# First modulation in quarters with the weights as stationary operand, and first key products over the channels in a fixed order

## The chip, the cores and the metric

The kernel runs on one core of a Trainium2 chip. TensorE multiplies (its weight loads are listed as PEld), VectorE (DVE), ScalarE (ACT) and GpSimd (POOL) do elementwise work, SyncE (SP) issues most DMAs. The metric is the device time in microseconds (us); lower is better. Three runs of the kernel before took 2928.11 to 2932.33 us, median 2929.12.

## What is computed

One layer of a diffusion backbone over 1024 tokens (64 x 16 grid) of 1024 channels, with 256 context tokens. The change touches the first step of all:

```python
def modulate(x, g, shift, scale):
    return rmsnorm(x, g) * (1 + scale) + shift

mod = silu(cond) @ ada_w + ada_b          # ada_w: 1024 x 6144; sh1, sc1, ... are 1024 columns each
h  = modulate(x,   norm1_g, sh1,  sc1)    # cond = c
hc = modulate(ctx, norm1_g, sh1c, sc1c)   # cond = c_ctx
p  = h @ w_in                             # columns 0 to 1023 are the keys
```

What follows (neighbourhood attention, Fourier and pooling mixers, gated merge, 16 experts of which each takes 128 tokens, final norm) is the same in both kernels.

## The kernel before

`start` (L179) brings everything up to the first key products. Its parts:

- *Modulation* (`modulation`, L216). The columns of shift and scale, 2048, come in four chunks of 512, each as two DMAs of 1 MB (rows of 2 KB). Both conditionings (`cs`, 2 columns) are done at once. In each half chunk, two of the four channel blocks go to TensorE with `cs` as stationary operand and 512 moving columns (L223), the other two are multiplied and summed on VectorE (L228, L230), and a matmul with ones (L233) adds these sums over the partitions. The result has 2 partitions, so it is copied (L235) and turned by four small transposes (L238) into one PSUM bank `mps` with the channels on the partitions. When all four chunks are done, L283 and L284 make `mod` (shift, scale) and `A` = g (1 + scale).
- *x* (`load`, `normed`). Four tiles of 128 tokens are loaded (L247), squared and summed on ScalarE (L249), scaled by their root mean square (L257) and turned by TensorE (L261), 4 transposes to each of the 8 channel blocks, two PSUM banks in rotation; ScalarE copies each bank out (L277, L289). This is done for each half of the tokens (x0 and x1). The four buffers `xt` serve both halves, so x1's loads wait for x0's transposes.
- *h* (`modulated`, L265). For each half and channel block k, `hT` gets a high part (L267, ScalarE) and a low part (L273, VectorE), from an unrounded value (L271, or ScalarE L269 for k = 2 and 5).
- *Keys* (`keys`, L309; `projT`, L300). For each half of the tokens and each of four blocks of 128 key columns, one PSUM bank gathers 8 channel blocks x 3 products (`mm3`: high x high, L67; high x low, L68; low x high, L69). A block therefore needs all eight channel blocks of `hT` before it can end. The weights come as two DMAs of 1 MB and are split into a high part on ScalarE (L62) and a low part; for this first chunk the low part is made on GpSimd.

A scheduler decides the order on every engine from the order of the program, its own estimate of times, and the buffers (three `wraw` for raw weights, four `whl` for split ones, two of which first hold the turned x). Each engine then keeps its order; SP issues DMAs in order too, so one that waits for a buffer holds those behind it.

Of the kernel before, what the change touches and what calls it, by code (L numbers as in the profile page):

```python
# [19 lines left out]
D = 1024  # L20
SEQ = 1024
# [13 lines left out]
def f(ap):  # L35
    return ap.bitcast(F32)


class Kernel:
# [75 lines left out]
    def run(self, upto=99):  # L115
        nc, tc, io = self.nc, self.tc, self.io
        with ExitStack() as st:
# [18 lines left out]
            self.queue = [lambda: self.wchunk(w_in, K_OFF, eng=nc.gpsimd)]  # L136
            self.queue += [cols(c) for c in (K_OFF + 512, V_OFF, V_OFF + 512, F_OFF, Q_OFF, Q_OFF + 512)]
# [3 lines left out]
            with ExitStack() as s1:  # L141
# [4 lines left out]
                self.hT = self.hpool.tile([128, 2, KT, SEQ], F32R, name="hT")  # L146
                with self.pool("kvq") as kvq:
                    self.hcT = kvq.tile([128, 2, KT, CTX], F32R, name="hcT")
                    self.keys_values(self.start())
# [29 lines left out]
    def start(self):  # L179
        nc, io = self.nc, self.io  # L180
        const, ps = self.const, self.ps
        with self.pool("startp", 2) as sp:
# [29 lines left out]
            ones = sp.tile([128, 3], F32, name="ones", bufs=1)  # L212
            nc.gpsimd.memset(ones, 0.0)
            nc.gpsimd.memset(ones[:, 1:2], 1.0)

            def modulation(ch):  # L216
                mp = ps.tile([128, 512], F32, name="mm")
                for hf in range(2):
                    raw = self.wraw.tile([128, 2048], F32, name="wraw")
                    rv = raw.rearrange("p (k c) -> p k c", c=512)  # L220
                    nc.sync.dma_start(rv, aw[:, 4 * hf:4 * hf + 4, 512 * ch:512 * ch + 512])
                    for k in range(2):
                        nc.tensor.matmul(mp[:2], cs[:, 4 * hf + k, :], rv[:, k],  # L223
                                         start=hf == k == 0, stop=False)
                    for w in range(2):
                        if hf == 0:
                            accs[w] = sp.tile([128, 512], F32, name=f"acc{w}", bufs=1)
                            nc.vector.tensor_scalar_mul(accs[w], rv[:, 2], cs[:, 2, w:w + 1])  # L228
                        for k in range(3 if hf == 0 else 2, 4):
                            nc.vector.scalar_tensor_tensor(accs[w], rv[:, k], cs[:, 4 * hf + k, w:w + 1], accs[w],  # L230
                                                           op0=ALU.mult, op1=ALU.add)
# [46 lines left out]
            for ch in range(1, 4):  # L278
                modulation(ch)
# [1145 lines left out]
```

## Time and profile before

| | us |
|---|---|
| median of 3 runs | 2929.12 |
| the profiled execution | 2928.25 |
| its span, first to last instruction | 2926.5 |
| first key product (L67) starts | 48.31 |
| TensorE turns to the context (first transpose of its tokens) | 100.20 |

A row of the timeline gives start, duration, engine, line, operation, output<-input and, in brackets, idle time of the engine before it and what ended it. A row with xN merges N instructions, and its duration runs from the first one's start to the last one's end. A matmul's own duration holds its latency, so the pitch between starts is what a product costs. An fp32 matmul is listed as two instructions, one of fp32r (the h and weight parts) as one.

### The profile page before, as it was taken

To read this page: it belongs to the slowest core of one execution; us is meant where nothing else is said; L and a number is where in the kernel's file an instruction comes from. 1 tells how busy PE (TensorE), PEld (TensorE's weight loads), DVE (VectorE), ACT (ScalarE), POOL (GpSimd) and SP (SyncE) were. 2 spreads that over 40 slices of the span, in tenths; PEclk is the share of its full clock that TensorE was granted. 3 is DMA by queue.
4 is the path that set the end of the run, shared out by engine and by line. 5 is a ranking of instruction groups with operands and counts; after the bars stand their busy time and mean duration, and the time that the engine had idled before them with its cause. 6 is when DMAs were issued, how large, how long until landed. Compare 5 with 4: busy or idle time off the path is not lost.

```text
span 2926.5 us, 36071 instructions
## 1 busy us (share of the span) xinstructions
PE 2811.0 (96%) x13607; PEld 2304.4 (79%) x13607; DVE 2040.7 (70%) x2412; ACT 1686.5 (58%) x2005; POOL 280.2 (10%) x436
## 2 busy tenths in 40 slices
PE   7999999999999789987999999999999999999996
PEld 3888888887788777766888888888888888888885
DVE  4423232245578773478888988888888888988887
ACT  5412122212078771245777777777777777777775
POOL 1110000001144320000000000000000000000000
PEclk9999999999999899998999999999999999999998
DMA  8433231225877748558999999999999999999994
GB/s 250 175 124 144 79 123 66 104 80 167 272 190 193 184 140 284 156 166 309 338 362 369 375 367 360 370 376 365 358 367 382 365 361 360 385 364 360 362 383 175
DMA packets 346351, 783.54 MB, mean 268 GB/s; under 512 B 17288, under 2 KB 61008, under 8 KB 346048
## 3 DMA queue, kind: packets, MB, share of 16 engines
q1 hardware_dynamic: 326272, 713.48, 69.3%
q0 software_dynamic: 19664, 67.60, 6.9%
q8 instruction: 107, 1.75, 0.2%
q14 instruction: 68, 0.56, 0.1%
q10 hardware_dynamic: 240, 0.16, 0.0%
HBM read 710.37 MB, written 70.80 MB: 267 GB/s over the span
## 4 chain that ended last, share of the span: by engine, by line
PE 46%; ACT 4%; DVE 2%; issue 1%; DMA 1%; DVEq 0%
PE y L69 5%; PE y L68 5%; PE y L67 5%; PE w_gate L69 5%; PE w_gate L68 5%; PE w_gate L67 5%; PE w_up L67 5%; PE w_up L69 5%; PE w_up L68 5%; ACT whl L62 2%; PE tp L1202 1%; ACT a L1132 1%; ACT xT L1128 1%; DMA wraw<-in_w_up 1%; PE tp L1101 0%
## 5 line engine op out<-in xcount | busy, mean ns | idle before, releaser
L63 DVE TENSOR_TENSOR whl<-wraw,whl 128x2048 fp32r<-128x2048 f32 (+1 forms) x656 | 1295.1, 1997 | 240.4 <-ACT whl L62 236.3
L62 ACT CAST whl<-wraw 128x2048 fp32r<-128x2048 f32 (+1 forms) x660 | 1092.1, 1671 | 445.0 <-PE y L69 132.5
L68 PE MATMUL mm<-hT,whl 128*128 128x512 f32 x768 | 300.9, 392 | 1.6 <-DVE hT L273 1.6
L67 PE MATMUL mm<-hT,whl 128*128 128x512 f32 x768 | 300.2, 392 | 1.5 <-ACT hT L267 1.5
L69 PE MATMUL mm<-hT,whl 128*128 128x512 f32 x768 | 300.8, 392 | 0.0
L69 PE MATMUL w_gate<-whl,xT 128*128 128x512 f32 (+1 forms) x768 | 290.8, 379 | 2.8 <-DVE xT L1133 2.8
L67 PE MATMUL w_gate<-whl,xT 128*128 128x512 f32 (+1 forms) x768 | 292.1, 380 | 0.0
L67 PE MATMUL w_up<-whl,xT 128*128 128x512 f32 (+1 forms) x768 | 291.5, 380 | 0.0
L68 PE MATMUL w_gate<-whl,xT 128*128 128x512 f32 (+1 forms) x768 | 289.7, 377 | 0.0
L69 PE MATMUL w_up<-whl,xT 128*128 128x512 f32 (+1 forms) x768 | 289.1, 376 | 0.0
L68 PE MATMUL w_up<-whl,xT 128*128 128x512 f32 (+1 forms) x768 | 288.4, 375 | 0.0
L67 PE MATMUL y<-whl,aT 128*128 128x512 f32 x704 | 284.8, 405 | 0.0
L69 PE MATMUL y<-whl,aT 128*128 128x512 f32 x704 | 278.7, 396 | 0.0
L68 PE MATMUL y<-whl,aT 128*128 128x512 f32 x704 | 278.1, 395 | 0.0
L67 PEld LDWEIGHTS mm<-hT,whl 128*128 128x128 f32 x768 | 144.9, 189 | 37.8 <-ACT sg L529 5.2
L69 PEld LDWEIGHTS w_gate<-whl,xT 128*128 128x128 f32 x768 | 145.2, 189 | 32.2 <-DVE xT L1133 3.5
L68 PEld LDWEIGHTS mm<-hT,whl 128*128 128x128 f32 x768 | 145.3, 189 | 31.7 <-DVE hT L273 2.1
L69 PEld LDWEIGHTS mm<-hT,whl 128*128 128x128 f32 x768 | 145.2, 189 | 30.1
L68 PEld LDWEIGHTS w_gate<-whl,xT 128*128 128x128 f32 x768 | 145.0, 189 | 29.6
L69 PEld LDWEIGHTS w_up<-whl,xT 128*128 128x128 f32 x768 | 144.5, 188 | 29.1
L67 PEld LDWEIGHTS w_gate<-whl,xT 128*128 128x128 f32 x768 | 144.8, 189 | 28.4
L68 PEld LDWEIGHTS w_up<-whl,xT 128*128 128x128 f32 x768 | 144.3, 188 | 28.3
(354 smaller groups left out, 4333.1 us busy)
## 6 DMA issues: line engine op xcount, KB each, us to landing
wraw<-in_w_gate SPq DMA_DIRECT2D x160, 1024.0 KB, 11.1
wraw<-in_w_up SPq DMA_DIRECT2D x160, 1024.0 KB, 9.0
wraw<-in_w_down SPq DMA_DIRECT2D x160, 1024.0 KB, 11.8
wraw<-in_w_in SPq DMA_DIRECT2D x28, 1024.0 KB, 5.5
wraw<-in_ada_w SPq DMA_DIRECT2D x24, 1024.0 KB, 6.3
wraw<-in_w_gate SPq DMA_DIRECT2D x32, 512.0 KB, 11.4
wraw<-in_w_up SPq DMA_DIRECT2D x32, 512.0 KB, 8.5
wraw<-in_w_down SPq DMA_DIRECT2D x32, 512.0 KB, 4.9
```

The lines of the kernel that those rows point to most:

```text
L62: self.nc.scalar.copy(hi, src)
L63: (eng or self.nc.vector).tensor_sub(lo, src, f(hi))
L67: mm(out, lh, rh, start=start, stop=False, **kw)
L68: mm(out, lh, rl, start=False, stop=False, **kw)
L69: mm(out, ll, rh, start=False, stop=stop, **kw)
L1128: nc.scalar.activation(ex.xT[:, 0, kk], tp[:, cs], AF.Identity, bias=B, scale=A)
L1132: nc.scalar.activation(h32[:, cs], tp[:, cs], AF.Identity, bias=B, scale=A)
L1202: nc.tensor.transpose(tp[:, 128 * k:128 * k + 128], ex.ready[:, 128 * k:128 * k + 128], self.ident)
```

## The change

The modulation is done by quarters. Quarter q holds shift and scale for two channel blocks, 2q and 2q+1: four DMAs of 512 KB (rows of 1 KB) instead of two of 1 MB. `affine(q)` multiplies with the 128x128 blocks of `ada_w` as stationary operand and the two columns of `cs` as moving one, 4 x 8 matmuls, straight into `mps` with the channels on the partitions. VectorE's sums, the ones, the copy and the small transposes are gone. `mod` and `A` of those two channel blocks follow at once. The quarters' raw data lie in places not yet in use: quarter 0 in `hcT`'s, 1 and 2 in the second half of `hT` (which becomes two tiles, class `Halves`), 3 in two `wraw` buffers.

x0 is loaded ahead of the weights. The key products of the first token half run over the channels: four PSUM banks are open together, and quarter q of the loop adds channel blocks 2q and 2q+1 to all four. After the second bank of quarters 0 to 2 the next `affine` stands, and x1's transposes stand in quarter 2. All this is fixed in the written order on TensorE (`manual_schedule`). The copies of turned x alternate between ScalarE and VectorE, as do the scalings; the low part of the first weights is made on VectorE.

```diff
--- before.py
+++ after.py
@@ -36,6 +36,21 @@
     return ap.bitcast(F32)
 
 
+class Halves:
+
+
+    def __init__(self, pool):
+        self.pool, self.tiles = pool, [None, None]
+
+    def take(self, half):
+        self.tiles[half] = self.pool.tile([128, 2, KT, 512], F32R, name=f"hT{half}")
+
+    def __getitem__(self, at):
+        p, s, k, t = at
+        half = t.start // 512
+        return self.tiles[half][p, s, k, t.start - 512 * half:t.stop - 512 * half]
+
+
 class Kernel:
 
 
@@ -133,8 +148,7 @@
-            self.queue = [lambda: self.wchunk(w_in, K_OFF, eng=nc.gpsimd)]
...
+                self.hT = Halves(self.hpool)
                 with self.pool("kvq") as kvq:
-                    self.hcT = kvq.tile([128, 2, KT, CTX], F32R, name="hcT")
-                    self.keys_values(self.start())
+                    self.keys_values(self.start(kvq))
...
-    def start(self):
+    def start(self, kvq):
...
-            ones = sp.tile([128, 3], F32, name="ones", bufs=1)
-            nc.gpsimd.memset(ones, 0.0)
-            nc.gpsimd.memset(ones[:, 1:2], 1.0)
-
-            def modulation(ch):
-                mp = ps.tile([128, 512], F32, name="mm")
+            mv = mps[:, :32].rearrange("p (c w) -> p w c", w=2)
+
+            def columns(q):
+
+
+                if q < 3:
+                    if q == 0:
+                        raw = kvq.tile([128, KT, 512], F32, name="hcT")
+                    else:
+                        raw = later[:, q - 1]
+                    parts = [raw[:, 0:4], raw[:, 4:8]]
+                else:
+                    parts = [self.wraw.tile([128, 2048], F32, name="wraw").rearrange("p (k c) -> p k c", c=512)
+                             for _ in range(2)]
                 for hf in range(2):
-                    raw = self.wraw.tile([128, 2048], F32, name="wraw")
-                    rv = raw.rearrange("p (k c) -> p k c", c=512)
-                    nc.sync.dma_start(rv, aw[:, 4 * hf:4 * hf + 4, 512 * ch:512 * ch + 512])
-                    for k in range(2):
-                        nc.tensor.matmul(mp[:2], cs[:, 4 * hf + k, :], rv[:, k],
-                                         start=hf == k == 0, stop=False)
-                    for w in range(2):
-                        if hf == 0:
-                            accs[w] = sp.tile([128, 512], F32, name=f"acc{w}", bufs=1)
-                            nc.vector.tensor_scalar_mul(accs[w], rv[:, 2], cs[:, 2, w:w + 1])
-                        for k in range(3 if hf == 0 else 2, 4):
-                            nc.vector.scalar_tensor_tensor(accs[w], rv[:, k], cs[:, 4 * hf + k, w:w + 1], accs[w],
-                                                           op0=ALU.mult, op1=ALU.add)
-                for w in range(2):
-                    nc.tensor.matmul(mp[:2], ones[:, 1 - w:3 - w], accs[w], start=False, stop=w == 1)
-                modr = sp.tile([2, 512], F32, name="modr", bufs=1)
-                nc.scalar.copy(modr, mp[:2])
+                    for s in range(2):
+                        c0 = D * s + 256 * q
+                        nc.sync.dma_start(parts[hf][:, :, 256 * s:256 * s + 256], aw[:, 4 * hf:4 * hf + 4, c0:c0 + 256])
+                return parts
+
+            def affine(q, parts):
+
                 for j in range(4):
-                    ct = 4 * ch + j
-                    nc.tensor.transpose(mps[:, 2 * ct:2 * ct + 2], modr[:, 128 * j:128 * j + 128],
-                                        self.ident[:2, :2])
-
-            accs = [None, None]
+                    ct = 8 * (j // 2) + 2 * q + j % 2
+                    for k in range(KT):
+                        nc.tensor.matmul(mps[:, 2 * ct:2 * ct + 2], parts[k // 4][:, k % 4, 128 * j:128 * j + 128],
+                                         cs[:, k], start=k == 0, stop=k == KT - 1)
+                both = lambda c: cols[:, c:c + 2].rearrange("p (o c) -> p o c", o=1).to_broadcast([128, 2, 2])
+                for o in (2 * q, 8 + 2 * q):
+                    nc.vector.tensor_add(mod[:, :, o:o + 2], mv[:, :, o:o + 2], both(o))
+                nc.vector.scalar_tensor_tensor(A[:, :, 2 * q:2 * q + 2], mod[:, :, 8 + 2 * q:10 + 2 * q], 1.0,
+                                               both(16 + 2 * q), op0=ALU.add, op1=ALU.mult)
 
             def load(src, n):
                 xs, ss = [], sp.tile([128, n], F32, name=f"ss{n}")
@@ -250,12 +265,19 @@
                     xs.append(xt)
                 return xs, ss
 
-            def normed(xs, ss, put):
+            def normed(xs, ss):
                 n = len(xs)
                 r = self.rstd(ss, sp, f"rs{n}")
                 for i in range(n):
-                    nc.scalar.activation(xs[i], xs[i], AF.Identity, scale=r[:, i:i + 1])
-                for k in range(KT):
+                    if i % 2:
+                        nc.vector.tensor_scalar_mul(xs[i], xs[i], r[:, i:i + 1])
+                    else:
+                        nc.scalar.activation(xs[i], xs[i], AF.Identity, scale=r[:, i:i + 1])
+                return xs
+
+            def turned(xs, ks, put):
+                n = len(xs)
+                for k in ks:
                     tp = ps.tile([128, 512], F32, name="tp", bufs=2)
                     for i in range(n):
                         nc.tensor.transpose(tp[:, 128 * i:128 * i + 128],
@@ -272,28 +294,72 @@
                                             op0=ALU.mult, op1=ALU.add)
                 (nc.gpsimd if k in () else nc.vector).tensor_sub(lo, h32, f(hi))
 
-            modulation(0)
+            wv = io["w_in"].rearrange("(k p) c -> p k c", p=128)[:, :, K_OFF:K_OFF + 512]
+            wr, wp = [], []
+
+            def wload(s):
+                wr.append(self.wraw.tile([128, 2048], F32, name="wraw"))
+                nc.sync.dma_start(wr[s].rearrange("p (k c) -> p k c", c=512), wv[:, 4 * s:4 * s + 4])
+
+            def wsplit(s):
+                hl = self.whl.tile([128, 2, 2048], F32R, name="whl")
+                for a in (0, 1024):
+                    self.split(hl[:, 0, a:a + 1024], hl[:, 1, a:a + 1024], wr[s][:, a:a + 1024])
+                wp.append(hl.rearrange("p s (k c) -> p s k c", c=512))
+
+            W = lambda s, k: wp[k // 4][:, s, k % 4]
+            put = lambda half: lambda k, p: (nc.vector.tensor_copy if k % 2 else nc.scalar.copy)(xn(k, half), p)
+            later = self.hpool.tile([128, 2, KT, 512], F32, name="hT1")
+            self.hT.take(0)
             x0 = load(lambda i: xv[i], 4)
-            normed(*x0, lambda k, p: nc.scalar.copy(xn(k, 0), p))
-            for ch in range(1, 4):
-                modulation(ch)
-            W = self.next(0)
-            mv = mps[:, :32].rearrange("p (c w) -> p w c", w=2)
-            for w in range(2):
-                nc.vector.tensor_add(mod[:, w, :], mv[:, w, :], cols[:, 0:16])
-                nc.vector.scalar_tensor_tensor(A[:, w, :], mod[:, w, 8:16], 1.0, cols[:, 16:24],
-                                               op0=ALU.add, op1=ALU.mult)
+            ada = [columns(0)]
+            wload(0)
+            ada.append(columns(1))
+            wload(1)
+
+            order = ExitStack()
+            order.enter_context(self.tc.manual_schedule(engines={mybir.EngineType.PE}))
+            affine(0, ada[0])
+            turned(normed(*x0), range(KT), put(0))
             x1 = load(lambda i: xv[4 + i], 4)
-            for half in range(2):
-                if half:
-                    normed(*x1, lambda k, p: nc.scalar.copy(xn(k, 1), p))
-                for k in range(KT):
-                    ts = slice(512 * half, 512 * half + 512)
-                    modulated(self.hT[:, 0, k, ts], self.hT[:, 1, k, ts], xn(k, half), k, 0)
-            for half in range(2):
-                self.keys(W, sp, 0, self.hT, 512 * half, 512, 512 * half)
+            ada += [columns(2), columns(3)]
+            wsplit(0)
+
+            acc = []
+
+            def shifted(q):
+                for k in (2 * q, 2 * q + 1):
+                    modulated(self.hT[:, 0, k, 0:512], self.hT[:, 1, k, 0:512], xn(k, 0), k, 0)
+
+            shifted(0)
+            x1 = normed(*x1)
+            for q in range(4):
+                for blk in range(4):
+                    if q == 0:
+                        acc.append(ps.tile([128, 512], F32, name="mm"))
+                    bs = slice(128 * blk, 128 * blk + 128)
+                    for k in (2 * q, 2 * q + 1):
+                        self.mm3(acc[blk], W(0, k)[:, bs], W(1, k)[:, bs],
+                                 self.hT[:, 0, k, 0:512], self.hT[:, 1, k, 0:512], k == 0, k == KT - 1)
+                    if blk == 1 and q < 3:
+                        affine(q + 1, ada[q + 1])
+                        shifted(q + 1)
+                        if q == 0:
+                            wsplit(1)
+                        if q == 2:
+                            turned(x1, range(4), put(1))
+                if q == 2:
+                    turned(x1, range(4, KT), put(1))
+                    self.hT.take(1)
+            for blk in range(4):
+                self.key_rows(sp, blk, acc[blk], 0)
+            for k in range(KT):
+                modulated(self.hT[:, 0, k, 512:1024], self.hT[:, 1, k, 512:1024], xn(k, 1), k, 0)
+            self.keys(W, sp, 0, self.hT, 512, 512, 512)
+            order.close()
             xc = load(lambda i: io["ctx"][128 * i:128 * i + 128], 2)
-            normed(*xc, lambda k, p: modulated(self.hcT[:, 0, k], self.hcT[:, 1, k], p, k, 1))
+            self.hcT = kvq.tile([128, 2, KT, CTX], F32R, name="hcT")
+            turned(normed(*xc), range(KT), lambda k, p: modulated(self.hcT[:, 0, k], self.hcT[:, 1, k], p, k, 1))
             return W
 
 
@@ -308,11 +374,13 @@
 
     def keys(self, W, sp, ch, src, t0, N, o0):
         for blk in range(4):
-            p = self.projT(W, blk, src, t0, N)
-            hl = sp.tile([128, 2, 512], F32R, name="khl", bufs=2)
-            self.split(hl[:, 0, :N], hl[:, 1, :N], p)
-            c0 = 512 * ch + 128 * blk
-            self.nc.gpsimd.dma_start(self.kd[c0:c0 + 128, :, o0:o0 + N], f(hl[:, :, :N]))
+            self.key_rows(sp, 4 * ch + blk, self.projT(W, blk, src, t0, N), o0)
+
+    def key_rows(self, sp, blk, p, o0):
+        N = p.shape[1]
+        hl = sp.tile([128, 2, 512], F32R, name="khl", bufs=2)
+        self.split(hl[:, 0, :N], hl[:, 1, :N], p)
+        self.nc.gpsimd.dma_start(self.kd[128 * blk:128 * blk + 128, :, o0:o0 + N], f(hl[:, :, :N]))
 
     def keys_values(self, W):
         nc, io = self.nc, self.io
```

TensorE at the start of the program, before (L223 and L233 are the modulation, L238 its turning, L261 transposes of x):

```order
L193 MATMUL mm<-ident,rows 128x48
L223 MATMUL mm<-wraw,cs 2x512 x4
L233 MATMUL mm<-acc_125,ones 2x512
L233 MATMUL mm<-acc_128,ones 2x512
L238 MATMUL mm<-ident,modr 128x2 x4
L223 MATMUL mm<-wraw,cs 2x512 x2
L261 MATMUL tp<-ident,xt 128x128 x2
L223 MATMUL mm<-wraw,cs 2x512
L261 MATMUL tp<-ident,xt 128x128 x2
L223 MATMUL mm<-wraw,cs 2x512
```

The same place after (L250 is `affine`, L283 transposes of x, L82 to L84 the three products of `mm3`; `hcT` is where quarter 0 lies, `hT_116` the first half of h):

```order
L206 MATMUL mm<-ident,rows 128x48
L250 MATMUL mm<-cs,hcT 128x2 x32
L283 MATMUL tp<-ident,xt 128x128 x32
L82 MATMUL mm<-hT_116,whl 128x512
L83 MATMUL mm<-hT_116,whl 128x512
L84 MATMUL mm<-hT_116,whl 128x512
```

The modulation was mixed with x's transposes; now one quarter and all 32 transposes stand ahead of the first product, and the other quarters behind it.

TensorE among the key products of the first half, before:

```order
L261 MATMUL tp<-ident,xt 128x128 x2
L69 MATMUL mm<-hT,whl 128x512
L67 MATMUL mm<-hT,whl 128x512
L68 MATMUL mm<-hT,whl 128x512
L69 MATMUL mm<-hT,whl 128x512
L261 MATMUL tp<-ident,xt 128x128 x8
L67 MATMUL mm<-hT,whl 128x512
```

And after, in the third quarter of the loop (`wraw` is where quarter 3 lies):

```order
L83 MATMUL mm<-hT_116,whl 128x512
L84 MATMUL mm<-hT_116,whl 128x512
L250 MATMUL mm<-cs,wraw 128x2 x32
L283 MATMUL tp<-ident,xt 128x128 x16
L82 MATMUL mm<-hT_116,whl 128x512
L83 MATMUL mm<-hT_116,whl 128x512
```

The transposes of x1 stood in groups of 2 to 8 between products; now 16 of them follow the 32 matmuls of a quarter without a product between, and a second 16 stand a little later.

SP's queue, before (L221 the modulation's weights, L247 x and context, L77 weights of `w_in`):

```order
L221 DMA wraw<-in_ada_w 128x4x512 x2
L247 DMA xt<-in_x 128x1x1024 x4
L221 DMA wraw<-in_ada_w 128x4x512 x6
L77 DMA wraw<-in_w_in 128x4x512
L247 DMA xt<-in_x 128x1x1024
L77 DMA wraw<-in_w_in 128x4x512
L247 DMA xt<-in_x 128x1x1024 x3
L77 DMA wraw<-in_w_in 128x4x512 x3
L247 DMA xt<-in_ctx 128x1024 x2
```

And after (L242 the quarters, L262 x and context, L302 and L92 weights of `w_in`; `hT_115` is the space of quarters 1 and 2):

```order
L262 DMA xt<-in_x 128x1x1024 x4
L242 DMA hcT<-in_ada_w 128x4x256 x4
L302 DMA wraw<-in_w_in 128x4x512
L242 DMA hT_115<-in_ada_w 128x4x256 x4
L302 DMA wraw<-in_w_in 128x4x512
L262 DMA xt<-in_x 128x1x1024 x4
L242 DMA hT_115<-in_ada_w 128x4x256 x4
L242 DMA wraw<-in_ada_w 128x4x256 x4
L92 DMA wraw<-in_w_in 128x4x512 x3
L262 DMA xt<-in_ctx 128x1024 x2
```

x0 moved ahead of all weights; quarters 2 and 3 stand behind x1.

## Rows read from the trace of the kernel before

**Rows 1.** The head of the page.

```profile
span 2926.5 us, 36071 instructions
```

**Rows 2.** Busy time by stage (windows); columns: stretch, length, busy of each engine, clock, DMA.

```profile
0.00:48.31 48.31, 31.42 (x98) 8.47 (x98) 22.34 (x46) 22.11 (x34) 4.06 (x10) 0.93 0.89 279
48.31:57.00 8.69, 7.08 (x19) 5.30 (x20) 3.91 (x5) 5.87 (x9) 5.96 (x3) 0.61 1.03 255
57.00:100.00 43.00, 43.00 (x207) 35.47 (x206) 24.86 (x46) 33.01 (x50) 5.36 (x8) 1.00 0.58 209
```

**Rows 3.** The timeline round the first key products and round the turn to the context.

```profile
48.31 1.20 PE L67 MATMUL mm<-hT,whl 128*128 128x512 f32 x4 [1.48 <-ACT hT L267]
...
51.12 0.79 PE L68 MATMUL mm<-hT,whl 128*128 128x512 f32 x1 [1.61 <-DVE hT L273]
...
92.04 0.39 PE L67 MATMUL mm<-hT,whl 128*128 128x512 f32 x1
...
92.72 0.39 PE L67 MATMUL mm<-hT,whl 128*128 128x512 f32 x1
...
100.20 0.60 PE L261 MATMUL tp<-ident,xt 128*128 128x128 f32 x4
```

**Rows 4.** Groups of TensorE by line and form, first 101 us.

```profile
L223 PE MATMUL mm<-wraw,cs 128*2 128x512 f32 x32 | 18.5, 703 | 0.8 <-DVE cs L202 0.8
```

**Rows 5.** The timeline at the router (L857) and transposes (L854), weight loads.

```profile
1213.71 0.97 PEld L857 LDWEIGHTS lg<-wm,x1T 128*128 128x128 f32 x8 [0.17 <-ACT x1T L855]
...
1214.51 0.29 PEld L854 LDWEIGHTS tp<-ident,x 128*128 128x128 f32 x2
```

**Rows 6.** The timeline and the window where eight pairs ran after idle time.

```profile
1324.37 1.78 PEld L1101 LDWEIGHTS tp<-tv,xg 128*128 128x128 f32 x8 [1.32 <-issue]
...
1324.20:1326.00 1.80, 1.60 (x8) 1.63 (x8) 0.65 (x2) 0.00 (x0) 0.00 (x0) 0.50 0.03 9
```

**Rows 7.** The timeline of the squares of x, and windows of the DMA.

```profile
11.99 1.06 ACT L249 ACTIVATE sq<-xt 128x1024 bf16<-128x1024 f32 x1 [3.44 <-DMA xt<-in_x]
...
18.56 1.06 ACT L249 ACTIVATE sq<-xt 128x1024 bf16<-128x1024 f32 x1 [1.06 <-DMA xt<-in_x]
...
4.00:8.00 4.00, 0.26 (x1) 0.18 (x1) 0.00 (x0) 0.56 (x1) 0.00 (x0) 1.00 1.05 393
...
12.00:16.00 4.00, 3.81 (x9) 0.60 (x7) 1.64 (x3) 2.29 (x4) 0.00 (x0) 1.00 1.04 246
```

**Rows 8.** Groups of VectorE and ScalarE by line and form, first 110 us.

```profile
L273 DVE TENSOR_TENSOR hT<-h,hT 128x512 fp32r<-128x512 f32 x16 | 10.7, 688 | 9.1 <-ACT h L269 7.4 <-ACT hT L267 1.5
L271 DVE TENSOR_SCALAR h<-whl,A,mod 128x512 f32<-128x512 f32 x12 | 8.7, 733 | 0.4 <-ACT whl L289 0.2
...
L63 DVE TENSOR_TENSOR whl<-wraw,whl 128x1024 fp32r<-128x1024 f32 x4 | 4.9, 1219 | 1.1 <-ACT whl L62 1.1
...
L267 ACT ACTIVATE hT<-whl,mod,A 128x512 fp32r<-128x512 f32 x16 | 12.4, 823 | 0.0
...
L277 ACT COPY whl<-tp 128x512 f32<-128x512 f32 x8 | 4.3, 589 | 4.6 <-PE tp L261 4.6
```

**Rows 9.** Windows round changes of the granted clock.

```profile
16.00:18.90 2.90, 0.00 (x0) 0.00 (x0) 0.00 (x0) 1.49 (x3) 0.00 (x0) 1.00 1.01 271
19.10:21.70 2.60, 0.00 (x0) 0.00 (x0) 0.58 (x4) 2.56 (x5) 0.00 (x0) 0.50 1.04 386
...
46.40:49.60 3.20, 1.60 (x8) 0.99 (x8) 2.70 (x5) 2.54 (x4) 3.20 (x2) 1.00 1.08 304
49.80:53.00 3.20, 1.88 (x5) 1.49 (x6) 2.42 (x5) 1.67 (x2) 0.55 (x1) 0.50 1.04 246
...
1299.00:1302.30 3.30, 2.62 (x19) 1.99 (x17) 1.67 (x4) 1.74 (x3) 0.52 (x1) 1.00 0.00 0
1302.50:1305.70 3.20, 1.06 (x8) 0.97 (x8) 1.41 (x8) 3.17 (x6) 0.00 (x0) 1.00 0.60 157
1305.90:1309.00 3.10, 0.58 (x2) 0.12 (x2) 2.09 (x13) 0.42 (x1) 1.01 (x2) 0.50 0.64 169
```

More of the change, by code (lines that the diff above doesn't have):

```diff
@@ L135, in run @@
             self.ready = []
-            self.queue = [lambda: self.wchunk(w_in, K_OFF, eng=nc.gpsimd)]
-            self.queue += [cols(c) for c in (K_OFF + 512, V_OFF, V_OFF + 512, F_OFF, Q_OFF, Q_OFF + 512)]
+            self.queue = [cols(c) for c in (K_OFF + 512, V_OFF, V_OFF + 512, F_OFF, Q_OFF, Q_OFF + 512)]
             self.queue += [lambda: self.wchunk(dft, 0), lambda: self.wchunk(wf, 0, 1024)]
@@ L145, in run @@
                 self.ps = s1.enter_context(self.pool("ps", 6, space=PSUM))
-                self.hT = self.hpool.tile([128, 2, KT, SEQ], F32R, name="hT")
+                self.hT = Halves(self.hpool)
                 with self.pool("kvq") as kvq:
-                    self.hcT = kvq.tile([128, 2, KT, CTX], F32R, name="hcT")
-                    self.keys_values(self.start())
+                    self.keys_values(self.start(kvq))
                 if upto < 1:
```

## The prediction

> **What bounds the kernel now.** I read the head of the page first, for the span [rows 1]; then the busy time by stage, for the place that the change touches [rows 2]; then the timeline round the first key products [rows 3]. The reader is to see three things. From 57 us on TensorE has no idle time at all: 43.00 of 43.00 us, at the full clock. What comes before is a chain that TensorE waits for (31.42 of 48.31 us busy), and its first key product starts at 48.31 us. Between them lies a bad stretch, 48.31 to 57, with the granted clock at 0.61 and an idle hole: four products start at 48.31, the next at 51.12.
>
> So the change is judged at one point: where TensorE has done the key products of both halves for the first 512 key columns, and turns to the context. That is 100.20 us in this execution [rows 3]. Behind it the order of TensorE is the same in both kernels, and TensorE is dense there, so what is won or lost at that point reaches the end whole. From 48.31 to 100.20 are 51.9 us: 192 products at 0.227 us (three take 92.72 - 92.04 = 0.68) are 43.6, the hole is 1.6, the half clock up to some 56.5 costs 2.7 (5.4 us at half speed), and 4.0 are left for the 32 transposes of the second half of x.
>
> **The change, part by part.**
>
> *Modulation on VectorE.* It goes, with 16 + 8 matmuls of 512 columns (the 16 direct ones show as 32 instructions, two for each fp32 matmul [rows 4]). All of it lies before 48.31, on the chain that is replaced, so its worth is in the new start, not in a sum of its own.
>
> *Modulation with the weights as stationary operand.* There are 4 quarters x 4 column blocks x 8 channel blocks = 128 fp32 matmuls, so 256 pairs of a weight load (128x128) and a matmul of 2 columns; 64 pairs to a quarter. Nothing in the trace has 2 columns against 128x128 weights, but the router is near: fp32 with 128x128 weights and 16 columns. Eight such pairs fill 1213.71 to 1214.51, 0.10 us a pair at the full clock, and they are bound by the load, as the columns are few [rows 5]. At half clock eight pairs with 4 columns took 1.78 us, 0.22 each [rows 6]; these are of another type, so I take 0.20, twice the router's. The bounds are 0.05 (if two columns let loads run closer than any row shows) and 0.227, a product's pitch. I take 0.10, the nearest row. A quarter is then 6.4 us of TensorE at the full clock, and quarters 1 to 3, which stand between key products, add 19.2 us to an engine that is the bound. Nothing hides them: the products behind them are in a fixed order.
>
> *The start.* x now goes ahead of the modulation weights. Before, its four tiles were squared at 11.99 to 18.56, 2.19 us apart, behind 2.1 MB of weights that came at 393 GB/s, 5.3 us [rows 7]. So the last lands near 13.2. Quarter 0, 2.1 MB in rows of 1 KB where 2 KB was read before, follows: 5.3 us at the weights' old rate, 8.5 at the 246 GB/s at which x came; I take 6, near the same tensor's row. Its third piece lands near 17.7, and 56 of the 64 pairs wait for that. TensorE has been idle, so its clock is low: 17.7 + 56 x 0.20 = 29 us; with a clock that recovers during the pairs, 26. Then come 32 transposes, which two PSUM banks tie to their copies: VectorE has 4 copies (0.59, by ScalarE's row), 2 scalings (0.73), 2 subtractions (0.69) and one weight split (1.22) before the first product can run [rows 8], 6.5 us and about 0.5 of handing over: 7. First product at 36, or at 33 with the better clock, against 48.31: 12.3 or 15.3 us won.
>
> The Trainium skill (Perfetto Trace Analysis, DMA Optimizations) says that transfers under 2 KB carry a considerable cost each, which speaks against the 1 KB rows. By it the quarter would lie at the slow end, 8.5 us. No row here has this tensor in such rows.
>
> *Products over the channels, fixed order.* The 96 products of the first half no longer wait for all eight channel blocks: the hole of 1.6 us goes. Each quarter's h has 12 products, 2.7 us, as cover; from a quarter's end to its h are three tiny VectorE operations, 0.82 on ScalarE and 0.69 on VectorE [rows 8], so that is hidden, and it is the next thing to be late if an engine is busy. The transposes of the second half stand in two lumps of 16, not spread through products: two banks and their copies hold TensorE some 2.2 us more (the third and fourth block of each lump wait for a copy of 0.6 that stands behind one or two activations of 0.82).
>
> *Moved on the queues.* On SP, x's second half waits until the transposes of the first have freed its four tiles, at about the first product, and quarters 2 and 3 wait behind it in the queue though their own space is free. With the start at 33, x takes 8.8 us, quarter 2 another 6, and its last pieces land near 51; TensorE wants them from 47 on (33, 24 products and a quarter of pairs, 5.4 + 6.4, and 12 more products, 2.7), and the first half of each block can run before: I count 1.6 us of wait. With the slower start nothing waits. The weight split's subtractions go from GpSimd (busy 5.96 us in the second stage [rows 2]) to VectorE, 4 x 1.22; two lie in the 7 us above, two under quarter 1. Bound: nothing, or 2.4 if VectorE is late there; I take nothing.
>
> **Sum with the clock held:** 33 + 43.6 + 4.0 + 2.2 + 19.2 + 1.6 = 103.6, against 100.20: 3.4 us slower. The earlier start is eaten by 19.2 us of weight loads.
>
> **The clock.** Does a quarter's 6.4 us of loads with two columns count as work? Rows show a clock of 1.00 that fell to 0.50 some 3 us after TensorE stopped (16.00 to 18.90 empty, then 0.50), and one that fell at 49.7 although four products ran at 48.31 [rows 9]. The mean of 0.61 over 8.69 us [rows 2] is 6.8 us at half speed, so it came back at 56.5, 5.4 us after the products resumed at 51.12. On the other side, 1299.0 to 1302.3, mostly transposes and eight router pairs, was followed by a clock still at 1.00; it fell only behind 1302.5 to 1305.7, which held eight pairs and nothing else [rows 9]. So a sparse stretch of pairs does not keep it, a denser mix does, and a dense stretch of pairs alone isn't there. I take it that it falls: two columns in a load of 128 keep the array nearly without data. For each of three quarters: the clock falls 3.8 us in (a choice between the 3 us above and the 6.4 of the quarter), so 26 of 64 pairs cost 0.10 more, 2.6; then the products run at half speed for about 4 us (5.4 above, with a slow first part), 2.0. With the first products at 36, also at half speed for 4 us: 3 x 4.6 + 2.0 = 15.8.
>
> The Trainium skill (TensorE: Matmul & The Clock Gate, Part 4) says that transposes do not count as TensorE being busy in the way matmuls do. The stretch of 1299 to 1302 held its clock with transposes in most of it, so the trace does not bear that out. By the rule, more of TensorE's small work would be idle time to the clock and the fall would be surer.
>
> **Forecast:** 36 + 43.6 + 4.0 + 2.2 + 19.2 + 15.8 = 120.8, so 20.6 us later. The profiled execution took 2928.25 us (span 2926.5 and 1.75 round it), 0.87 under the median of 2929.12; 2928.25 + 20.6 + 0.87 = 2949.7, or 2950.
>
> **Rivals.**
> 1. The clock holds through the quarters. For it: the mix at 1299. Against it: eight pairs alone did not hold it. 2929.1 + 3.4 = 2932.5. The Trainium skill (TensorE: Matmul & The Clock Gate, Part 1) has the clock follow how busy TensorE has lately been; taken plainly, loads back to back are busy, and it gives this case.
> 2. Faster: the pairs run closer than the router's, in the three inner quarters. With the clock held the change gains below 0.100 - 3.4/192 = 0.082 us a pair; at 0.05 it is 9.6 less, 6.2 us faster, 2923. For it: 2 columns against 16. Against it: no row shows loads of 128 columns closer than the router's 0.10.
> 3. The quarters land slowly (8.5 us each), with the clock held: the start is 2 later and quarters 2 and 3 keep TensorE waiting some 3 more: 2937. For it: x came at 246 GB/s, not 393. Against it: the queue has 6 us of slack per quarter once pairs stand between products.
> That the change doesn't do what it says is out for the order, which is fixed on TensorE as written.
>
> **How the numbers follow.** The forecast has 0.55, the held clock 0.27, the slow quarters 0.08, faster pairs 0.10. What this kernel's measurement can tell from no change is about 0.2%, 5.9 us. The forecast alone spans 2943 to 2957 (2 to 7 us a quarter for the clock). The range must reach the held clock: 2930 to 2957, with about 0.11 left out below and 0.07 above. Faster by over 0.2% is the better part of rival 2: 0.06. Within: rival 1, the rest of rival 2, some of 3: 0.30. Slower: 0.64.
>
> **What would show it.** The first key product near 36 us (33 with a held clock); 64 pairs in 6.4 us where the clock is 1.00, about 9 where it drops; the granted clock under 1.00 in each of the three quarters' second halves and in the products behind them; the turn to the context near 121 us (104 in rival 1). A pitch of pairs under 0.08 us, or a turn to the context before 100, would make it wrong; so would a first product later than 42, which would put the cause in the loads.

## The result and the profile after

The changed kernel takes 2949.02 us (median of 4 runs, 2946.50 to 2949.71) against 2928.61 for the kernel before, measured beside it (4 runs, 2926.67 to 2932.33): ratio 1.0067, 95% interval 1.0051 to 1.0083. It is 20.4 us slower; the forecast was 2950. The profiled execution took 2946.5 us, 18.25 over that of before.

The head of the page, which answers to [rows 1]:

```profile
span 2944.7 us, 36430 instructions
```

The stages of the changed kernel, cut at its own first key product and turn to the context, answer to [rows 2] (the columns are the same):

```profile
0.00:36.50 36.50, 20.54 (x96) 18.99 (x97) 8.19 (x22) 16.14 (x23) 0.70 (x6) 1.00 0.79 235
36.50:57.00 20.50, 20.50 (x120) 18.66 (x118) 6.83 (x11) 8.45 (x13) 0.00 (x0) 0.83 0.99 274
57.00:100.00 43.00, 42.76 (x211) 38.40 (x211) 19.44 (x42) 19.79 (x30) 1.82 (x2) 0.72 0.37 127
100.00:120.40 20.40, 20.40 (x91) 16.86 (x90) 8.79 (x16) 6.94 (x12) 3.44 (x5) 1.00 0.72 258
```

From 36.5 us on TensorE is idle for 0.24 us in all, so nothing in this stretch is a wait: all that was lost is TensorE's own work, longer or slower. From 57 to 100 us it is as busy as before (42.76 of 43.00) at a clock of 0.72 where it had 1.00. VectorE and ScalarE, which had 24.86 and 33.01 us of work there, now have under 20 each, so neither is what TensorE waits for.

The timeline of TensorE answers to [rows 3]. Columns: start, length of the group, what ran, its count.

```profile
17.34 12.11 PE L250 MATMUL mm<-cs,hcT 128*128 128x2 f32 x56 [1.08 <-DMA hcT<-in_ada_w]
29.31 6.03 PE L283 MATMUL tp<-ident,xt 128*128 128x128 f32 x28
...
36.53 0.48 PE L82 MATMUL mm<-hT,whl 128*128 128x512 f32 x1
...
39.38 9.02 PE L250 MATMUL mm<-cs,hT 128*128 128x2 f32 x64
48.26 0.77 PE L82 MATMUL mm<-hT,whl 128*128 128x512 f32 x1
...
55.23 11.02 PE L250 MATMUL mm<-cs,hT 128*128 128x2 f32 x64
66.11 0.77 PE L82 MATMUL mm<-hT,whl 128*128 128x512 f32 x1
...
74.29 9.72 PE L250 MATMUL mm<-cs,wraw 128*128 128x2 f32 x64
83.87 3.85 PE L283 MATMUL tp<-ident,xt 128*128 128x128 f32 x16
87.37 0.78 PE L82 MATMUL mm<-hT,whl 128*128 128x512 f32 x1
...
90.88 1.03 PE L283 MATMUL tp<-ident,xt 128*128 128x128 f32 x8
...
93.11 0.48 PE L82 MATMUL mm<-hT,whl 128*128 128x512 f32 x1
...
120.44 0.60 PE L283 MATMUL tp<-ident,xt 128*128 128x128 f32 x4
```

The first key product starts 11.8 us earlier than before, and the turn to the context comes at 120.44 against 100.20, 20.2 us later. Between them stand three quarters of 8.9, 10.9 and 9.6 us, each of 64 pairs with no idle time in it or behind it. Windows round the changes of the granted clock answer to [rows 9]:

```profile
39.50:44.30 4.80, 4.80 (x46) 4.80 (x45) 0.00 (x0) 0.00 (x0) 0.00 (x0) 1.00 1.04 245
44.60:48.10 3.50, 3.50 (x18) 3.50 (x18) 0.00 (x0) 0.00 (x0) 0.00 (x0) 0.50 1.03 248
48.30:51.20 2.90, 2.90 (x8) 2.32 (x9) 1.63 (x5) 2.23 (x4) 0.00 (x0) 0.50 1.10 349
55.40:58.00 2.60, 2.60 (x25) 2.60 (x25) 0.17 (x1) 2.33 (x5) 0.00 (x0) 1.00 1.10 348
58.20:66.00 7.80, 7.80 (x38) 7.80 (x38) 2.21 (x7) 2.19 (x2) 0.00 (x0) 0.50 0.48 170
66.20:71.70 5.50, 5.50 (x14) 4.34 (x14) 2.32 (x6) 2.23 (x3) 0.00 (x0) 0.50 0.01 1
74.40:78.40 4.00, 4.00 (x39) 4.00 (x37) 0.00 (x0) 0.00 (x0) 0.00 (x0) 1.00 0.00 0
78.70:83.80 5.10, 5.10 (x25) 5.10 (x26) 0.00 (x0) 0.00 (x0) 0.00 (x0) 0.50 0.11 12
```

The weight loads (second pair of columns) fill each stretch of pairs, 4.80 of 4.80 us and so on. At a clock of 1.00, 45 loads take 4.80 us: 0.107 a pair. At 0.50, 38 take 7.80: 0.205. The clock fell from 2.4 to 1.2 GHz (1.00 to 0.50) inside each of the three quarters, 5.1, 2.9 and 4.3 us after its start, and stayed low behind it: through 7 key products, through 13, and after the third quarter through 16 transposes and 3 products.

What was won and lost up to the turn, from these rows: the start -11.8; the hole of before -1.6 and its half clock -2.7; 192 pairs at 0.107 +20.5; half clock +15.4 (8.8 in the pairs: 29.3 us in place of 20.5; 5.3 in the products: 27.1 for the first 96 against 21.8 for the second; 1.3 in 16 transposes: 3.50 us at 83.87 against 2.23 for the 16 at 90.88); lumps of transposes +0.5. Sum +20.3, against 20.2 measured.

### The profile page after: what moved, and what is told of

The parts are those of the page before. It is cut to its first block, busy times and chain, and to the rows that moved or that the text cites. A ratio compares the mean times of both kernels' runs of the same rounds, so it can differ in the third digit from the quotient of the medians.

```text
span 2944.7 us, 36430 instructions
## 1 busy us (share of the span) xinstructions
PE 2833.8 (96%) x13799; PEld 2349.4 (80%) x13799; DVE 2034.3 (69%) x2405; ACT 1676.3 (57%) x1989; POOL 270.6 (9%) x430
## 4 chain that ended last, share of the span: by engine, by line
PE 46%; ACT 4%; issue 2%; DVE 1%; DMA 1%; DVEq 0%
PE y L84 5%; PE y L82 5%; PE y L83 5%; PE w_gate L84 5%; PE w_gate L82 5%; PE w_gate L83 5%; PE w_up L82 5%; PE w_up L84 5%; PE w_up L83 5%; ACT whl L77 2%; PE tp L1270 1%; ACT a L1200 1%; ACT xT L1196 1%; PE tp L1169 0%; DVE a L1264 0%
## 5 line engine op out<-in xcount | busy, mean ns | idle before, releaser
L77 ACT CAST whl<-wraw 128x2048 fp32r<-128x2048 f32 (+1 forms) x660 | 1092.2, 1671 | 437.0 <-PE y L84 132.3
L82 PE MATMUL mm<-hT,whl 128*128 128x512 f32 x768 | 303.2, 395 | 0.0
L84 PE MATMUL mm<-hT,whl 128*128 128x512 f32 x768 | 301.3, 392 | 0.0
L82 PE MATMUL w_gate<-whl,xT 128*128 128x512 f32 (+1 forms) x768 | 293.4, 382 | 0.0
L84 PE MATMUL w_gate<-whl,xT 128*128 128x512 f32 (+1 forms) x768 | 290.3, 378 | 2.8 <-DVE xT L1201 2.8
L82 PE MATMUL w_up<-whl,xT 128*128 128x512 f32 (+1 forms) x768 | 292.1, 380 | 0.0
L84 PE MATMUL w_up<-whl,xT 128*128 128x512 f32 (+1 forms) x768 | 289.3, 377 | 0.0
L82 PE MATMUL y<-whl,aT 128*128 128x512 f32 x704 | 285.4, 405 | 0.0
L84 PE MATMUL y<-whl,aT 128*128 128x512 f32 x704 | 278.6, 396 | 0.0
L82 PEld LDWEIGHTS mm<-hT,whl 128*128 128x128 f32 x768 | 146.1, 190 | 36.3 <-ACT sg L597 5.2
L84 PEld LDWEIGHTS w_gate<-whl,xT 128*128 128x128 f32 x768 | 145.2, 189 | 32.9 <-DVE xT L1201 3.5
L84 PEld LDWEIGHTS mm<-hT,whl 128*128 128x128 f32 x768 | 145.5, 189 | 30.5
L84 PEld LDWEIGHTS w_up<-whl,xT 128*128 128x128 f32 x768 | 144.5, 188 | 29.4
L82 PEld LDWEIGHTS w_gate<-whl,xT 128*128 128x128 f32 x768 | 144.9, 189 | 28.3
## 6 DMA issues: line engine op xcount, KB each, us to landing
wraw<-in_w_up SPq DMA_DIRECT2D x160, 1024.0 KB, 10.7
```

Of the source, the lines that this page charges most:

```text
L77: self.nc.scalar.copy(hi, src)
L82: mm(out, lh, rh, start=start, stop=False, **kw)
L84: mm(out, ll, rh, start=False, stop=stop, **kw)
```

## Experiments

The theory: TensorE bounds the stretch, the pairs put 0.107 us of weight load each on it, and with two columns moving in each the clock falls. The rivals: the new fixed order costs the time; the data come late; the loads alone do it and the width of the moving operand is of no account. Nine kernels were run. The kernel before, run beside them, had a median of about 2929 us each time.

**Wide moving operand.** The vector is repeated to 64 columns, so that a pair has the same weight load with 64 columns in place of 2.

```diff
+            csw = sp.tile([128, KT, 64], F32, name="csw", bufs=1)
...
-                        nc.tensor.matmul(mps[:, 2 * ct:2 * ct + 2], parts[k // 4][:, k % 4, 128 * j:128 * j + 128],
-                                         cs[:, k], start=k == 0, stop=k == KT - 1)
+                        nc.tensor.matmul((mps, cps)[ct // 8][:, 64 * (ct % 8):64 * (ct % 8) + 64],
+                                         parts[k // 4][:, k % 4, 128 * j:128 * j + 128],
+                                         csw[:, k], start=k == 0, stop=k == KT - 1)
```

> The changed kernel, but every matmul of a quarter has 64 moving columns (the two of cs, 32 times over) instead of 2; the weight loads are the same, and only two of the 64 result columns are used. Theory (loads of 128 columns set the pitch; with 2 columns the array gets next to no data, and this lets the granted clock fall): the pitch stays near 0.107 us at the full clock, the clock holds at 1.00 in quarters 1 to 3, the turn to the context comes at 105 to 109 instead of 120.4, the median near 2935. Rival (the clock falls because weight loads themselves count for little, whatever the matmuls behind them carry, or because of the waits round the quarters): the clock still falls in each quarter, turn at 119 or later, 2949 or more.

Measured: 2937.74 us, ratio 1.0035 (1.0022 to 1.0048), turn at 111.29. The timeline of TensorE:

```profile
17.32 12.21 PE L253 MATMUL mm<-csw,hcT 128*128 128x64 f32 x56 [0.98 <-DMA hcT<-in_ada_w]
29.33 6.00 PE L287 MATMUL tp<-ident,xt 128*128 128x128 f32 x28
...
36.51 0.48 PE L82 MATMUL mm<-hT,whl 128*128 128x512 f32 x1
...
38.59 0.50 PE L83 MATMUL mm<-hT,whl 128*128 128x512 f32 x1 [0.90 <-DVE hT L299]
...
40.55 7.25 PE L253 MATMUL mm<-csw,hT 128*128 128x64 f32 x64
```

and the stages:

```profile
36.00:50.00 14.00, 12.99 (x90) 11.70 (x91) 5.85 (x10) 6.71 (x12) 0.00 (x0) 1.00 0.90 227
50.00:75.00 25.00, 23.76 (x167) 21.15 (x166) 6.30 (x17) 7.05 (x11) 0.00 (x0) 1.00 0.51 168
75.00:100.00 25.00, 22.67 (x117) 18.84 (x117) 21.39 (x39) 19.83 (x31) 3.08 (x4) 1.00 0.69 241
```

Sixty-four columns cost next to nothing in a pair (7.25 us for 64 are 0.11 each, against 0.107), and the clock held at 1.00 through all three quarters. So the fall comes from what the pairs move, not from the loads as such, and it is worth 9.2 us at the turn. The expected turn, 105 to 109, was missed by 2 us: with TensorE faster, 4.5 us of idle time appear (2.1 for hT, as at 38.59, and 2.3 for copies of turned x), which the half clock had covered.

**An eighth of the pairs.** Quarters 1 to 3 multiply only their first channel block.

```diff
+                    n = 1 if q else KT
-                    for k in range(KT):
+                    for k in range(n):
...
```

> The changed kernel without seven eighths of the matmuls of quarters 1 to 3 (only the first channel block is multiplied, so the modulation of those channels is not the reference's): 8 pairs a quarter instead of 64; all loads, waits and the order stay. Theory (the pairs on TensorE and the low clock behind them are the whole loss): 26 us of pairs and some 5 us of slow products go, the turn to the context comes near 90 and the median near 2919, about 10 us under the kernel before. Rival (the fixed order makes TensorE wait for VectorE, ScalarE or late quarters, and the pairs only fill the time of these waits): the pairs are replaced by idle time, turn at 105 or later, 2934 or more.

Measured: 2923.52 us, ratio 0.9984 (0.9974 to 0.9994), turn at 95.41. So leaving out 168 pairs gains 25.0 us at the turn, in place of the 31 expected. The saving fell short because quarter 2 of the weights is now late:

```profile
49.09 0.89 PE L251 MATMUL mm<-cs,hT 128*128 128x2 f32 x4 [3.50 <-DMA hT<-in_ada_w]
...
50.60 1.02 PE L251 MATMUL mm<-cs,hT 128*128 128x2 f32 x4 [0.61 <-DMA hT<-in_ada_w]
```

These two waits are 4.1 us. Behind the first of them the clock was at 0.50 from 49.3 to 56.1 us, with only 8 pairs in that stretch, and this took some 3 more. The rival is out, since the pairs did not turn into idle time of their own length. Even with most of the modulation left out the kernel is only 0.16% faster than before.

**Quarter 0 ahead of x.** The load of x's first half goes behind that of the first quarter.

```diff
+            ada = [columns(0)]
             x0 = load(lambda i: xv[i], 4)
-            ada = [columns(0)]
```

> The changed kernel with quarter 0 loaded ahead of x instead of behind it. Theory (the start is set by quarter 0's landing plus 64 pairs at the half clock, with the transposes of x behind them in the fixed order): the pairs run while x still comes, the transposes then wait for x (scaled near 24.5), the first key product moves from 36.5 to near 32, the turn to 116, the median near 2945. Rival (x is needed first, since its squares and scaling are the longer chain): the first product does not come before 36, 2949.

Measured: 2945.37 us, ratio 1.0064 (1.0047 to 1.0081), first product at 33.30, turn at 117.38. Each number stands within 1.5 us of what was expected: late data set the start, and loading them first is worth 3.1 us at the turn. More was not tried; the transposes wait for x now.

**Free order.** The fixed order on TensorE is taken away, and the scheduler orders its instructions.

```diff
             order = ExitStack()
-            order.enter_context(self.tc.manual_schedule(engines={mybir.EngineType.PE}))
```

> The changed kernel without the fixed order on TensorE: the scheduler places the same instructions. Theory (pairs and clock, not the order): the pairs cost the same, but the scheduler mixes them with products and transposes, so the clock falls less often; turn to the context at 112 to 120, median 2941 to 2949, still slower than before. Rival (the fixed order is what loses the time): turn near 100 or earlier, 2929 or less.

Measured: 2956.88 us, ratio 1.0096 (1.0080 to 1.0113), turn at 127.67. The expectation was missed, for the theory and the rival alike: the free order is 7 us later at the turn than the written one. Its timeline where the 64 pairs of quarter 1 run:

```profile
37.11 0.95 PE L250 MATMUL mm<-cs,hT 128*128 128x2 f32 x8
...
40.05 3.63 PE L250 MATMUL mm<-cs,hT 128*128 128x2 f32 x32
...
45.45 5.12 PE L250 MATMUL mm<-cs,hT 128*128 128x2 f32 x24
```

and the stages behind it:

```profile
50.00:75.00 25.00, 22.54 (x98) 20.07 (x98) 7.80 (x17) 12.18 (x18) 0.00 (x0) 0.64 0.52 171
75.00:100.00 25.00, 25.00 (x124) 22.58 (x124) 6.86 (x17) 9.31 (x14) 0.00 (x0) 0.65 0.13 43
```

The same two windows of the changed kernel have a clock of 0.70 and 0.80. The scheduler puts these pairs in groups of 8, 32 and 24 between a few products; the clock fell at 44.5 all the same, as it did in the written order, and was low for longer behind it; 2.46 us of idle time came besides. So the fixed order isn't what costs time.

**Wide, and weights earlier.** The wide kernel with quarter 0 ahead of x, and quarter 2 ahead of x's second half.

```diff
+            ada = [columns(0)]
             x0 = load(lambda i: xv[i], 4)
-            ada = [columns(0)]
...
+            ada += [columns(2)]
+            wsplit(0)
             x1 = load(lambda i: xv[4 + i], 4)
-            ada += [columns(2), columns(3)]
-            wsplit(0)
+            ada += [columns(3)]
```

> The changed kernel with 64 moving columns in the quarters (as before), quarter 0 loaded ahead of x, and quarter 2 loaded ahead of the second half of x. Theory (three separate costs: the pairs, the clock, the late start): the gains of the two single edits add, 9 us from the clock and 3 from the start, and the wait for quarter 2 stays away: turn to the context at 106 to 109, median 2934 to 2937, still slower than before, as 192 pairs at 0.107 us, 20.5 us, remain. Rival (the start and the clock overlap, since the same products follow both): turn at 111 or later.

Measured: 2934.59 us, ratio 1.0020 (1.0008 to 1.0031), turn at 108.46, as expected. The two gains add, and the kernel is still slower than before: with the clock held, 192 pairs at about 0.11 remain.

**Operand swap undone, new order kept.** The vector is the stationary operand again and the weights move, 512 columns at a time; half of the channel blocks are summed on VectorE. Quarters, fixed order and x first stay as changed; the transposes of x's first half stand round the sums of quarter 0.

```diff
-                    for k in range(KT):
-                        nc.tensor.matmul(mps[:, 2 * ct:2 * ct + 2], parts[k // 4][:, k % 4, 128 * j:128 * j + 128],
-                                         cs[:, k], start=k == 0, stop=k == KT - 1)
+                    nc.tensor.transpose(mps[:, 2 * ct:2 * ct + 2], modr[:, 128 * j:128 * j + 128], self.ident[:2, :2])
...
+                    if blk == 0 and q < 3:
+                        direct(q + 1, ada[q + 1])
+                        modr = summed(q + 1, sums(q + 1, ada[q + 1]))
```

> The operand swap alone undone: new loads, quarters and fixed order as in the changed kernel, but each quarter is multiplied as before (cs as stationary operand, 512 moving columns, half of the channel blocks summed on VectorE, then turned). Theory (the swap is the loss, the new order and start are a gain): a quarter costs 12 instructions of 0.43 and four small transposes, 5.5 us in place of 6.9, and keeps the clock at 1.00; start near 32, turn at 99 to 104, median 2928 to 2933. Rival (quarters between the products cost as much in any form, as VectorE is late with sums or with h): turn at 112 or later, 2941 or more.

Measured: 2931.98 us, ratio 1.0014 (1.0003 to 1.0025), first product at 30.55, turn at 105.23. Undoing the swap, with the order that the sums need, thus brings back 15.2 of the 20.2 us: 6.0 at the start, since quarter 0 is now 8 instructions from 16.07 to 22.02 us in place of 64 pairs to 29.31, and 9.2 behind it. The turn missed the expected 99 to 104 by little, for waits of 5.5 us, three of them here:

```profile
40.56 0.41 PE L277 MATMUL mm<-ident,modr 2*128 2x2 f32 x4 [0.32 <-ACT modr L271]
...
46.14 0.50 PE L83 MATMUL mm<-hT,whl 128*128 128x512 f32 x1 [1.99 <-DVE hT L321]
...
48.20 0.73 PE L83 MATMUL mm<-hT,whl 128*128 128x512 f32 x1 [0.68 <-DVE hT L321]
```

The clock did not quite hold at 1.00 either: behind these waits it was at 0.50 from 48.3 to 51.7 us.

**The same with weights earlier**, as in the wide kernel, and then **with three quarters of the channel blocks on VectorE** (`ND = 3` for `ND = 2`).

> As the kernel with the swap undone, and quarter 0 loaded ahead of x, quarter 2 ahead of the second half of x. Theory: the first product is set by x alone (scaled near 24.5 us, then 7 us of transposes and h), so near 32 to 33, and no quarter is waited for: turn at 98 to 101, median 2926 to 2930. Rival (VectorE's sums, 5.4 us a quarter, delay h): turn at 104 or later.

> As the one before, with three quarters of the channel blocks summed on VectorE instead of half: TensorE's part of a quarter falls from 12 to 8 instructions of 0.43 us, 5.1 to 3.4, VectorE's rises from 5.4 to 8.4. Theory (TensorE's time inside the loop is what counts): turn 3 to 5 us earlier than with half, 94 to 97, median 2922 to 2926, faster than both kernels. Rival (VectorE is then the late one, with sums and h in one queue): turn not earlier than with half.

Measured: 2934.93 (ratio 1.0019, 1.0009 to 1.0028; first product at 35.42, turn at 106.92) and 2935.53 (1.0021, 1.0012 to 1.0031; turn at 109.20). The first is a miss. The turn lies where the rival put it, but VectorE is the smaller part of that: the waits for h behind the first product are 1.8 us. More was lost at the start, 35.42 in place of 32 to 33. The turned x was scaled near 24.5 as expected, but TensorE had by then been idle for 10.7 us, its clock was at 0.50 until 29.6, and the transposes ran at that clock. In the second VectorE is late, as its rival had it:

```profile
43.15 1.88 PE L269 MATMUL mm<-acc,ones 128*2 128x512 f32 x4 [1.19 <-DVE acc L263]
...
58.28 3.35 PE L269 MATMUL mm<-acc,ones 128*2 128x512 f32 x4 [2.75 <-DVE acc L263]
```

**Swap undone, sums ahead of time.** The direct products and sums of quarters 2 and 3 stand before the loop quarter that wants them, their weights are loaded ahead of x's second half, and the transposes of that half are spread, two channel blocks to a bank. (What the text on record calls x's first tile of the context is x's second half.)

```diff
+                if 0 < q < 3:
+                    direct(q + 1, ada[q + 1])
+                    modr = summed(q + 1, sums(q + 1, ada[q + 1]))
...
-                        if q == 2:
-                            turned(x1, range(4), put(1))
+                    if q == 2:
+                        turned(x1, (2 * blk, 2 * blk + 1), put(1))
```

> The operand swap undone (the vector is stationary again and the weights move 512 columns, half of the channel blocks summed on VectorE), the new order kept, and the order changed once more: quarters 2 and 3 of the weights are loaded ahead of x's first tile of the context, the direct products and sums of quarters 2 and 3 stand ahead of the first bank of the loop quarter in which they are wanted, and the transposes of that tile are spread over the banks of loop quarter 2, two channel blocks at a time. Theory (without the swap the pairs are few and the clock holds; what was left in the run with the swap undone were waits for VectorE and for copies, which the spreading covers): first product at about 30.5 us, some 5.6 us for each inner quarter, the turn at about 97 us, so a time of about 2926 us (2924 to 2930). Rival (VectorE has more to do than these stretches hold, so that its sums come late wherever they stand): the turn at 104 us or later and a time of 2931 us or more.

Measured: 2927.52 us, ratio 0.9993 (0.9984 to 1.0003), first product at 30.68, turn at 97.24: what the theory said, and no difference from before that can be measured. Groups of TensorE from 30 to 98 us (count, busy time, mean ns, idle time before):

```profile
L252 PE MATMUL mm<-hT,cs 128*2 128x512 f32 x16 | 7.2, 592 | 0.0
L269 PE MATMUL mm<-acc,ones 128*2 128x512 f32 x12 | 5.6, 592 | 0.0
...
L252 PE MATMUL mm<-wraw,cs 128*2 128x512 f32 x8 | 3.6, 592 | 0.0
L277 PE MATMUL mm<-ident,modr 2*128 2x2 f32 x12 | 1.2, 202 | 0.0
```

TensorE waits for nothing here but 0.94 us, at a clock of 1.00. Yet a start 17.6 us earlier than before gives a turn only 3.0 us earlier, since the modulation of three quarters, 17.6 us of busy time (7.2 + 5.6 + 3.6 + 1.2; counted from start to start, 16.7), now stands between key products. That uses up the earlier start. The 3.0 us come from what the kernel before lost behind its first product, a hole of 1.6 us [rows 3] and 2.7 us by the half clock [rows 2], less small losses here. Before, the modulation lay ahead of the first product, where TensorE was idle for 16.9 of 48.31 us [rows 2].

## Why the prediction was right

*The place.* Turn forecast at 120.8, measured 120.44. Behind the turn nothing was to change: 2824.3 us are left in the profile after (2944.7 - 120.44) and 2826.3 before. These 2 us in the other direction are why the profiled execution is 18.25 slower and not 20.2. They are no effect that can be told from chance: in the profiles of the nine experiments the part behind the turn took 2821.0 to 2829.6 us.

*The start.* 36 forecast, 36.53 measured. The third piece of quarter 0 was put at 17.7 (17.34), the pairs' end at 29 (29.31; 0.214 us a pair in the half clock, forecast 0.20), the transposes and their chain at 7 (7.2). The clock column reads 1.00 there, since the first change that the trace holds is the rise at 34.2; the pitch tells that it was low. The rise was earlier than forecast, so the first products ran at full clock: 0.1 us lost, not 2.0.

*The pairs.* The router's 0.10 was the right row; 0.107 makes 20.5 and not 19.2. The faster pairs of rival 2 did not show.

*The clock.* 15.4 measured, 15.8 forecast, but made up a little otherwise: 8.8 in the pairs (forecast 7.8), 5.3 in the products (8.0 with the first ones), 1.3 in transposes, which were not thought of. That the width of the moving operand decides was a guess in the prediction, and the wide kernel showed it: the same loads, a held clock. Rival 1, with the clock held, gave 2932.5 and a turn at 103.6; the wide kernel, which is that case made real behind the first product, took 2937.74, with the turn at 111.29. Most of these 7.7 us have a name: its start stayed at 36.51 and not 33, since quarter 0 ran at the half clock there too (3.5); 192 pairs took 21.2 and not 19.2 (2.0); TensorE waited 2.1 us for h, which the sum did not have; and the wait of 1.6 for quarter 2 did not come. Its waits for copies, 2.3 us, are the 2.2 of the sum.

*The rest.* The transposes of the second half were put at 6.2, the clock apart, and took 4.4: the first lump ran at the half clock, which covered its copies, and the second waited 0.24 us for one, where 2.2 were forecast for both. No wait for quarter 2, none for the weight split on VectorE, as taken.

*Mechanism and luck.* Every part of the mechanism showed: the earlier start, 64 pairs a quarter in full on TensorE, the clock falling in each quarter. That the turn came within 0.4 us is luck: the start was 0.5 late and the pairs 1.3 dearer, the transposes were 1.8 cheaper and the clock 0.4.

*The loads.* In the rows 48.30 to 51.20 and 55.40 to 58.00 above, quarters 2 and 3 come alone, at 349 and 348 GB/s, where the same tensor in rows of 2 KB came at 393 before [rows 7]. At 348 the 2.1 MB of a quarter take 6.0 us, as the prediction took, and rival 3 had no part.

The Trainium skill (Perfetto Trace Analysis, DMA Optimizations) has transfers under 2 KB pay a considerable cost each; the trace agrees in the direction, and 348 against 393 GB/s, 11% less, is its size for rows of 1 KB here.

## What to carry to other kernels

Work that moves from a stretch in which the bounding engine waits into one in which it is dense costs its full length there, however early that lets the dense stretch begin: here a start 17.6 us earlier was used up by about 17 us of such work, and the 3.0 us that were left came from a hole and a low clock that the new order avoids. A matmul that loads 128 x 128 weights for two columns costs its weight load, and many in a row cost the clock as well, for themselves and for the products behind them; price both from rows at either clock. And where a slow engine covers waits, count these before you forecast what its speeding up will give: of the 15.4 us that the low clock cost, holding it gave back 9.2 at the turn.

## What the runs showed of the hardware

A weight load of 128 x 128 in fp32 sets the pair's pitch up to 64 columns at least: 0.107 us with 2 columns, 0.110 with 64, at the full clock. Sixty-four columns held the clock at 1.00 but did not raise it: quarter 0 of the wide kernel ran 56 pairs in 12.0 us, 0.214 each, to its end. The rise came in both kernels during the transposes behind it (34.2 and 34.3 us), which TensorE did without a gap:

```profile
29.40:34.10 4.70, 4.70 (x22) 3.78 (x22) 2.91 (x8) 2.75 (x5) 0.00 (x0) 1.00 0.02 6
```

This window of the changed kernel holds transposes alone, 22 in 4.70 us, 0.214 each, twice the 0.109 at which those from 90.88 on follow each other; behind them the clock was at its upper level. The Trainium skill (TensorE: Matmul & The Clock Gate, Part 4) says that transposes do not count as busy in the way matmuls do; the trace does not bear that out. These are transposes by a matmul with the identity. In the kernel with the swap undone 8 matmul instructions with 512 moving columns, from 16.07 to 22.02 us, raised it too, at 21.0. Why these and the transposes raised it and 56 pairs with 64 columns did not stays open.
